# Block two's mixer takes its Fourier half first, then k and v, then q in two halves; the first loads and block one's convolution change order too

## The chip, the cores and the metric

The kernel runs on one core of one Trainium2 chip. The metric is the device time in microseconds (us), the median of several runs. A profile of one execution shows, for each engine, when each instruction ran. The engines are TensorE (PE for its matmuls, PEld for its weight loads), VectorE (DVE), ScalarE (ACT), GpSimd (POOL) and SyncE (SP, which here only issues transfers).

## The reference

256 tokens of width 1024 go through two blocks of two layers each, in float32:

```python
for l in range(2):                                   # block one
    x = x + 0.5 * swiglu_ffn(rmsnorm(x), ...)
    x = x + mixer(rmsnorm(x), ...)                   # GLU + 31-tap convolution + layer norm, three kinds of windowed attention, gates
    x = x + 0.5 * swiglu_ffn(rmsnorm(x), ...)
    x = rmsnorm(x)
for l in range(2):                                   # block two
    p = rmsnorm(x) @ w_in                            # u (512), q (8 heads of 64), k and v (2 heads each)
    y_f = real(fft2(u)) @ w_f + b_f
    y_a = windowed_gqa(rope(rmsnorm(q)), rope(rmsnorm(k)), v, sink)
    x = x + concat(rmsnorm(y_f), rmsnorm(y_a)) @ w_o
    up = conv3(rmsnorm(x) @ w_up)
    x = x + (silu(gate) * val) @ w_down
```

## The kernel before, in words

**Weights as a stream of units.** All weights lie in HBM in the order in which they are used, cut into units of 128 x 1024 (`weight_stream`, `make_units`). `fetch` issues a unit's transfer on SP's queue into one of four `raw` buffers. `ahead` splits a unit in two float32r parts: `wh`, a copy by ACT (line 334), and `wl`, the rest, by DVE (line 335), up to three units ahead of use. `unit` hands the next one out. Each product is three matmuls: `wl` with the high part of the activations, `wh` with the high part, `wh` with the low part.

**Products.** `token_major` computes 256 tokens x 512 columns: four units, and in each two blocks of 128 rows for two token tiles, so 48 matmuls of 512 columns into two PSUM banks (`acc`, a pool of four banks). `mid` is a dictionary: after unit q the functions in `mid[q]` are traced. `evac` is called for token tile 0 and then for tile 1. A second pool of four banks (`aux`) takes transposes, sums, scores. The FFN's products are the same (`ffn1`): `gate(c - 1)` after a product's second unit, its transposes (`turn`) after the fourth, and in the second product the sums of squares (`norm`) after the first unit.

**Order of the work.** The program is traced in Python order, and a scheduler then orders each engine's queue at compile time by what it expects to be ready; each engine works through its queue in order. `issue_after(ins)` keeps what is traced inside it, on the engine of `ins`, behind `ins` in that queue (no wait for its end).

**Start.** `run` issues the transfers of x's eight blocks, with four units in between, and 8 warm-up matmuls. `add(b)` splits block b of x (ACT `xh`, DVE `xl`) and adds its square to a sum (`square_add`: ACT squares, DVE adds). `ahead(-2)` splits one unit behind block 0.

**Block one's mixer.** 13 products of `token_major`: four for the GLU, nine for q, k, v of the three groups. `evac` of q and k reads a PSUM bank (line 868) and runs `head_norm_rope` at once (eight squares with accumulator reads on ACT, a `pow` on POOL, four DVE operations of 512 columns), then the other tile does the same. The transposes of a product follow one product later. The convolution stands between the products: `conv_forward` (lines 786 to 799; three `acc` banks per half), `conv_inverse` (lines 809 to 819; two `acc` banks per half), then mean and variance. Then ten steps of attention with sixteen half units of the gates between them; in each step `scores` (line 897) come first, and `norm_mean`, `norm_cols`, `norm_rows` stand behind steps 1, 3 and 4. Temporaries of 512 columns (`t2`) share nine buffers; bias rows (`brow`) are among them.

**Block two's mixer (`mixer2`).** First q, by `token_major` (`evac_q`, `head_norm_rope` for each tile with eight heads); then u by `token_major`, with the residual's normalisation (`residual`, eight DVE operations, line 1389) after its second unit; then k and v, 48 matmuls of 256 columns (lines 1079 to 1081). Then `f1` (the Fourier transform over the tokens, two halves), the transposes of q and k (`transpose_to`, line 667), and four steps of attention, each with one head of keys and one token tile: `soft` issues the scores (line 1207) and the softmax, `fill` gives what is put between (`f2`, `f3`, the output projection `proj`).

## Time and profile before

| | us |
|---|---|
| median of 3 runs | 1929.17 |
| lowest and highest run | 1925.79, 1930.48 |
| the profiled execution | 1923.16 |
| its span, first to last instruction | 1921.4 |
| mean granted TensorE clock (1 is 2.4 GHz) | 0.996 |

The profile page lists each engine's busy time and the costliest groups of instructions; the trace behind it gives every instruction's start, duration and the idle time of its engine ahead of it, with the instruction whose end released it. Times in rows count from the start of the span. L335 is line 335 of the kernel.

### The profile page before, as it was taken

The numbers are of one execution on the slowest core, as the hardware profiler recorded it, in microseconds if no ns is written. First come the engines' busy times: TensorE is split into PE (matmuls) and PEld (weight loads), VectorE is DVE, ScalarE is ACT, GpSimd is POOL, SyncE is SP. The second block draws the span as 40 slices with busy tenths as digits, with TensorE's granted clock in tenths as the row PEclk, the third lists the DMA queues.
The fourth block names the chain that finished last, engine by engine and source line by source line (L and its number), as shares of the span: only waits on it lengthen the run. The fifth ranks groups of instructions, "written<-read, shape, count | busy, mean of one in ns | idle before, by whom it ended". The sixth has DMA issues, their size and how long they took to land.

```text
span 1921.4 us, 29776 instructions
## 1 busy us (share of the span) xinstructions
PE 1893.8 (99%) x11240; PEld 1656.0 (86%) x11240; DVE 1344.3 (70%) x2232; ACT 1105.9 (58%) x2087; POOL 116.8 (6%) x109
## 2 busy tenths in 40 slices
PE   8999999999999999999999999999989999999999
PEld 6888878899988888888788999888879998879999
DVE  5655687967655566656879776655779985679873
ACT  5554545666544555545457575444677664677652
POOL 1000012300000000000123000000100000100000
PEclk8999999999999999999999999999999999999999
DMA  7655655434555555546555345556434655425553
GB/s 231 218 192 182 212 181 171 163 112 165 187 186 185 183 193 182 196 178 210 182 174 161 122 158 183 187 186 210 136 123 144 213 201 193 165 100 175 197 179 120
DMA packets 95792, 337.99 MB, mean 176 GB/s; under 512 B 11270, under 2 KB 13926, under 8 KB 95520
## 3 DMA queue, kind: packets, MB, share of 16 engines
q1 hardware_dynamic: 91584, 325.97, 49.5%
q0 software_dynamic: 2944, 8.11, 1.8%
q10 hardware_dynamic: 1120, 2.00, 0.3%
q8 instruction: 88, 1.44, 0.3%
q14 instruction: 56, 0.46, 0.1%
HBM read 334.99 MB, written 1.05 MB: 175 GB/s over the span
## 4 chain that ended last, share of the span: by engine, by line
PE 84%; issue 8%; DVE 4%; POOL 2%; DMA 1%; ACT 1%; ACTq 0%; POOLq 0%; DVEq 0%
PE acc L683 11%; PE acc L685 10%; PE acc L684 10%; PE acc L352 10%; PE acc L354 9%; PE acc L353 9%; PE acc L513 5%; PE acc L515 5%; PE acc L514 5%; POOL rs L643 2%; PE pt L1018 1%; PE ht L592 1%; DVE wl L335 1%; PE s L897 1%; PE acc L1169 1%
## 5 line engine op out<-in xcount | busy, mean ns | idle before, releaser
L335 DVE TENSOR_TENSOR wl<-raw,wh 128x1024 fp32r<-128x1024 f32 (+1 forms) x618 | 749.2, 1215 | 405.4 <-ACT wh L334 404.6
L334 ACT ACTIVATE wh<-raw 128x1024 fp32r<-128x1024 f32 (+1 forms) x618 | 647.7, 1052 | 574.9 <-PE acc L685 269.3
L683 PE MATMUL acc<-wl,xh 128*128 128x512 f32 x1184 | 470.3, 397 | 6.6 <-DVE wl L335 4.1
L685 PE MATMUL acc<-wh,xl 128*128 128x512 f32 x1184 | 463.0, 391 | 0.0
L684 PE MATMUL acc<-wh,xh 128*128 128x512 f32 x1184 | 462.1, 390 | 0.0
L683 PEld LDWEIGHTS acc<-wl,xh 128*128 128x128 f32 x1184 | 223.3, 189 | 54.1 <-DVE wl L335 4.9
L685 PEld LDWEIGHTS acc<-wh,xl 128*128 128x128 f32 x1184 | 222.9, 188 | 48.0 <-DVE xl L364 0.2
L684 PEld LDWEIGHTS acc<-wh,xh 128*128 128x128 f32 x1184 | 223.6, 189 | 44.2
L513 PE MATMUL acc<-wl,hh 128*128 128x512 f32 x440 | 172.4, 392 | 0.0
L352 PE MATMUL acc<-xn,wl 128*128 128x256 f32 x608 | 172.1, 283 | 0.0
L353 PE MATMUL acc<-xn,wh 128*128 128x256 f32 x608 | 172.1, 283 | 0.0
L354 PE MATMUL acc<-xn,wh 128*128 128x256 f32 x608 | 172.1, 283 | 0.0
L515 PE MATMUL acc<-wh,hl 128*128 128x512 f32 x440 | 171.3, 389 | 0.0
L514 PE MATMUL acc<-wh,hh 128*128 128x512 f32 x440 | 171.2, 389 | 0.0
L352 PEld LDWEIGHTS acc<-xn,wl 128*128 128x128 f32 x608 | 116.7, 192 | 0.0
L353 PEld LDWEIGHTS acc<-xn,wh 128*128 128x128 f32 x608 | 116.7, 192 | 0.0
L354 PEld LDWEIGHTS acc<-xn,wh 128*128 128x128 f32 x608 | 116.7, 192 | 0.0
L352 PE MATMUL acc<-xh,wl 128*128 128x256 f32 x352 | 103.8, 295 | 0.0
L353 PE MATMUL acc<-xh,wh 128*128 128x256 f32 x352 | 100.1, 284 | 0.0
L354 PE MATMUL acc<-xl,wh 128*128 128x256 f32 x352 | 100.0, 284 | 0.0
L515 PEld LDWEIGHTS acc<-wh,hl 128*128 128x128 f32 x440 | 82.6, 188 | 17.4
L514 PEld LDWEIGHTS acc<-wh,hh 128*128 128x128 f32 x440 | 82.7, 188 | 16.7
(278 smaller groups left out, 2969.2 us busy)
## 6 DMA issues: line engine op xcount, KB each, us to landing
raw<-wts SPq DMA_DIRECT2D x606, 512.0 KB, 3.3
brow<-b_in POOLq DMA_DIRECT2D x26, 256.0 KB, 3.9
raw<-wts SPq DMA_DIRECT2D x8, 384.0 KB, 3.3
fw<-dft SPq DMA_DIRECT2D x4, 512.0 KB, 5.7
tab<-tab ACTq DMA_DIRECT2D x1, 1024.0 KB, 8.4
out<-xn SPq DMA_DIRECT2D x8, 128.0 KB, 3.4
wraw<-conv_w POOLq DMA_DIRECT2D x6, 124.0 KB, 4.7
raw<-dft SPq DMA_DIRECT2D x2, 258.0 KB, 2.6
```

The lines of the kernel that those rows point to most:

```text
L334: nc.scalar.activation(h[:, :n], r[:, :n], AF.Copy)
L335: nc.vector.tensor_tensor(lo[:, :n], r[:, :n], h[:, :n].bitcast(F32), op=ALU.subtract)
L352: mm(out, wl, xh, start=start, stop=False, **k)
L353: mm(out, wh, xh, start=False, stop=False, **k)
L354: mm(out, wh, xl, start=False, stop=stop, **k)
L513: mm(accs[t], hh[:, ts], wl[:, c], start=k == 0, stop=False)
L514: mm(accs[t], hh[:, ts], wh[:, c], start=False, stop=False)
L515: mm(accs[t], hl[:, ts], wh[:, c], start=False, stop=k == NF - 1)
L643: nc.gpsimd.tensor_tensor(rs[:, :nh], vv[:, :nh], self.mhalf[:, :nh], op=ALU.pow)
L683: mm(accs[t], xh[k][:, ts], wl[:, c], start=k == 0, stop=False)
L684: mm(accs[t], xh[k][:, ts], wh[:, c], start=False, stop=False)
L685: mm(accs[t], xl[k][:, ts], wh[:, c], start=False, stop=k == KB - 1)
```

## The change

Block two's mixer: the first product is u, with the sums and the tables' transfer inside; then k and v, both token tiles in one `aux` bank (`product`), with `f1` behind them; then q in two halves of 256 columns (key head 0, key head 1), each again a `product` of 48 matmuls of 256 columns, with `f2` inside the first. `norm_rope` norms and rotates both token tiles at once (one square on ACT, one `tensor_reduce` on DVE, one `pow`), `turn` transposes both tiles into one bank. `f3(0)`, `f3(1)` and the transposes of k and of q's first half stand ahead of the attention; `f3(2)`, `f3(3)` are step 0's fill, q's second transposes step 1's. The residual goes to step 4, behind the last softmax on DVE. The weight stream is reordered to match.

Elsewhere: 14 warm-up matmuls; an ACT table load at the very start; units 1 and 2 split between x's blocks; the squares of x behind the first product's third unit; `norm` and `gate(0)` one unit later in every FFN's second product; what `mid` issues on TensorE pinned behind the unit's last matmul; in block one's mixer both tiles read out of PSUM before either is normed, `conv_forward`'s first two accumulators and `conv_inverse`'s two in `aux`, the norm's sums in `acc`, a gate ahead of the first scores, and the convolution's norm one and two steps later, on DVE and ACT behind the step's softmax.

```diff
-WARM = 8
+WARM = 14
...
-        parts += [_wide(w[:, 512:1024]), _wide(w[:, :512]), w[:, 1024:].reshape(2, 4, P, 256).transpose(0, 2, 1, 3)]
+        parts += [_wide(w[:, :512])] + [w[:, c:c + 256].reshape(2, 4, P, 256).transpose(0, 2, 1, 3) for c in (1024, 512, 768)]
...
     def follow(self, x, gains, scales=(None,)):
-        def add(b):
+        def add(b, both=True):
             for dst, part in zip(o, self.operand(x[b:b + 1], gains[b:b + 1], b)):
                 dst += part
+            if both:
+                square(b)
+
+        def square(b):
             for i, sc in enumerate(scales):
                 sums[i] = self.square_add(sums[i], x[b], **({} if sc is None else dict(scale=sc[b])))
...
     def ffn1(...)
-            mid = {0: tail} if c == 0 else {1: [lambda: gate(c - 1)], 3: [lambda: turn(c - 1)]}
+            mid = {2 if first else 0: tail} if c == 0 else {1: [lambda: gate(c - 1)], 3: [lambda: turn(c - 1)]}
             if c == 1:
-                mid[0] = [norm]
+                mid = {1: [norm], 2: [lambda: gate(0)], 3: [lambda: turn(0)]}
...
     def token_major(self, o, evac, mid={}):
-            for f in mid.get(q, ()):
-                f()
+            if q in mid:
+                with self.tc.issue_after(last.ins):
+                    for f in mid[q]:
+                        f()
-        for t in range(2):
-            evac(t, accs[t])
+        for f in [evac(t, accs[t]) for t in range(2)]:
+            if f is not None:
+                f()
...
     def conv_forward():
-                    a = self.acc()
+                    a = self.acc() if len(parts) == 2 else self.aux("U")
     def conv_inverse(half):
-            parts = [self.acc(), self.acc()]
+            parts = [self.aux("inv"), self.aux("inv")]
...
         def norm_mean():
+            with self.tc.issue_after(stat["soft"].ins), self.tc.issue_after(stat["exp"].ins):
...
                 z = self.t2("z")
                 nc.vector.scalar_tensor_tensor(z, a, r[:, t:t + 1], row, op0=ALU.mult, op1=ALU.add)
                 i = which * 3 + g
-                self.head_norm_rope(z, NH, cg[:, t, i], sg_[:, t, i], z)
                 turn.append(lambda d=dst: self.transpose_to(z, 4, d, t))
+                return lambda: self.head_norm_rope(z, NH, cg[:, t, i], sg_[:, t, i], z)
...
-        later = {1: norm_mean, 3: norm_cols, 4: norm_rows}
+        later = {2: norm_mean, 5: norm_cols, 6: norm_rows}
         for i in range(len(steps) + 2):
+            if i == 0:
+                gate(*gates.pop(0))
+                for f in held:
+                    f()
             if i < len(steps):
                 j, t = steps[i]
                 soft0 = (j, t, soft(t, scores(t, j)))
             gate(*gates.pop(0))
-            if i == 0:
-                for f in held:
-                    f()
...
     def mixer2(...)
+        def product(mid={}):
+            xh, xl = o
+            a = self.aux("pr")
+            for u in range(2):
+                wh, wl = self.unit(1024)
+                for kk in range(4):
+                    k = u * 4 + kk
+                    c = slice(kk * 256, (kk + 1) * 256)
+                    for t in range(2):
+                        out, ts = a[:, t * 256:(t + 1) * 256], slice(t * P, (t + 1) * P)
+                        mm(out, xh[k][:, ts], wl[:, c], start=k == 0 and t == 0, stop=False, skip_group_check=True)
+                        mm(out, xh[k][:, ts], wh[:, c], start=False, stop=False, skip_group_check=True)
+                        last = mm(out, xl[k][:, ts], wh[:, c], start=False, stop=k == KB - 1, skip_group_check=True)
+                if u in mid:
+                    with self.tc.issue_after(last.ins):
+                        for f in mid[u]:
+                            f()
+            return a
+
+        def norm_rope(z, nh, i, out, dup=1):
...
+            nc.scalar.activation(sq, z, AF.Square)
+            nc.vector.tensor_reduce(ss, heads(sq), axis=mybir.AxisListType.X, op=ALU.add)
...
+            nc.gpsimd.tensor_tensor(rs, vv, self.mhalf[:, :n], op=ALU.pow)
...
+            tt(A_, A_, B_, op=ALU.add)
...
+                tt(o4[:, :, u], heads(A_), rs[:, :, None].to_broadcast([P, n, HD]), op=ALU.mult)
+
+        def turn(z, dst):
+            p = self.aux("tr")
+            for i in range(2):
                 for t in range(2):
+                    nc.tensor.transpose(p[:, i * 256 + t * P:i * 256 + (t + 1) * P], z[:, t * 256 + i * P:t * 256 + (i + 1) * P], self.ident)
+            nc.scalar.activation(dst, p.rearrange("p (i c) -> p i c", i=2), AF.Copy)
...
+        def resid():
+            with self.tc.issue_after(cell["soft"]):
+                x.extend(residual())
+
+        fill = {0: [lambda: f3(2), lambda: f3(3)], 1: [lambda: turns[2](), later("s", lambda: self.square_sum([yf[:, b] for b in range(4)]))],
+                2: [lambda: proj(0, 0, 0), later("c", lambda: self.rms_cols(cell["s"], 512))], 3: [lambda: proj(0, 0, 1)],
+                4: [lambda: (fourier_part(0), proj(0, 1, 0)), resid], 5: [lambda: proj(0, 1, 1)]}
...
+        self.token_major(o, lambda t, a: self.split(a, uh[t], ul[t], st["rc"][:, t:t + 1]), {0: tail, 2: [tables], 3: [start]})
+        a = product({1: [lambda: f1(0), lambda: f1(1)]})
...
+        norm_rope(z[:, :256], 2, 1, zk, dup=2)
+        turns = [lambda: turn(zk, kT[:, :2])]
+        for i, mid in enumerate(({0: [lambda: f2(0)], 1: [lambda: f2(1)]}, {})):
+            a = product(mid)
+            zq = self.t2("z")
+            nc.scalar.activation(zq, a, AF.Copy)
+            norm_rope(zq, 4, 0, zq)
+            turns.append(lambda i=i, zq=zq: turn(zq, qT[:, i * 2:i * 2 + 2]))
+        f3(0)
+        f3(1)
+        for f in turns[:2]:
             f()
...
     def run(self):
         nc.scalar.dma_start(self.vec[:, :KB], self.a["vec"][:, :KB])
+        nc.scalar.activation(self.small("tbl", 1), self.mhalf[:, :1], AF.Copy)
...
         for b in range(KB):
-            if b == 1:
-                self.ahead(-2)
-            add(b)
+            add(b, False)
+            if b % 2 and b < 6:
+                self.ahead(b // 2 - 2)
```

## Rows read from the trace of the kernel before

**Rows 1.** Page: busy us (share) xinstructions; two groups: busy, mean ns, idle before.

```profile
PE 1893.8 (99%) x11240; PEld 1656.0 (86%) x11240; DVE 1344.3 (70%) x2232; ACT 1105.9 (58%) x2087; POOL 116.8 (6%) x109
...
L335 DVE TENSOR_TENSOR wl<-raw,wh 128x1024 fp32r<-128x1024 f32 (+1 forms) x618 | 749.2, 1215 | 405.4 <-ACT wh L334 404.6
L334 ACT ACTIVATE wh<-raw 128x1024 fp32r<-128x1024 f32 (+1 forms) x618 | 647.7, 1052 | 574.9 <-PE acc L685 269.3
```

**Rows 2.** Timeline, TensorE, behind `conv_inverse`, layer 0: start, duration, [idle before <-releaser].

```profile
305.61 0.39 PE L685 MATMUL acc<-wh,xl 128*128 128x512 f32 x1
307.11 0.50 PE L683 MATMUL acc<-wl,xh 128*128 128x512 f32 x1 [1.11 <-DVE z L868]
307.45 0.39 PE L684 MATMUL acc<-wh,xh 128*128 128x512 f32 x1
307.68 0.40 PE L685 MATMUL acc<-wh,xl 128*128 128x512 f32 x1
```

**Rows 3.** Timeline, TensorE, inside k and v's product.

```profile
1388.62 0.28 PE L1079 MATMUL acc<-wl,xh 128*128 128x256 f32 x1
1388.74 0.28 PE L1080 MATMUL acc<-wh,xh 128*128 128x256 f32 x1
```

**Rows 4.** Timeline of the first 24 us (q behind an engine: it issues).

```profile
1.05 3.78 PE L1358 MATMUL warm<-ones 128*128 128x128 f32 x16 [1.05 <-DVE ones L242]
...
7.52 0.50 PE L683 MATMUL acc<-wl,xh 128*128 128x512 f32 x1 [2.69 <-DVE wl L335]
...
8.06 15.29 SPq L322 DMA_DIRECT2D raw<-wts  x7
...
15.06 1.01 PE L433 MATMUL sumc<-ones,sacc 128*128 128x1 f32 x4 [2.93 <-DVE sacc L383]
...
17.47 0.79 PE L683 MATMUL acc<-wl,xh 128*128 128x512 f32 x1 [1.40 <-DVE wl L335]
```

**Rows 5.** Windows, first product: length, busy (instructions) by engine, PEclk, DMA share, GB/s.

```profile
7.52:27.76 20.24, 15.92 (x52) 12.62 (x53) 12.49 (x21) 10.74 (x19) 4.05 (x5) 0.75 0.80 259
```

**Rows 6.** Groups of TensorE, 262 to 402 us (block one's mixer, layer 0).

```profile
L683 PE MATMUL acc<-wl,xh 128*128 128x512 f32 x126 | 50.2, 398 | 1.3 <-DVE z L868 1.1 <-DVE yt L797 0.2
...
L897 PE MATMUL s<-qkv,qkv 64*128 64x128 f32 (+1 forms) x60 | 6.9, 329 | 2.3 <-ACT qkv L668 1.9 <-ACT pT L1020 0.4
...
L786 PE MATMUL acc<-uh,wl 128*128 128x512 f32 (+1 forms) x8 | 3.5, 440 | 0.9 <-DVE Y L794 0.7 <-DVE qkv L865 0.2
```

**Rows 7.** Groups of TensorE, 1377 to 1420 us (block two's mixer, layer 0).

```profile
L1079 PE MATMUL acc<-wl,xh 128*128 128x256 f32 x16 | 4.6, 289 | 0.9 <-DVE wl L335 0.9
...
L352 PE MATMUL acc<-yfh,wl 128*128 128x256 f32 x12 | 3.4, 291 | 2.7 <-ACT yfh L360 2.7
...
L667 PE MATMUL tr<-ident,zk 128*128 128x128 f32 x4 | 0.8, 293 | 2.0 <-DVE zk L660 2.0
```

**Rows 8.** Groups of TensorE, 1670 to 1700 us (block two's mixer, layer 1).

```profile
L352 PE MATMUL acc<-yfh,wl 128*128 128x256 f32 x16 | 4.7, 304 | 1.1 <-ACT yF L1135 1.1
...
L667 PE MATMUL tr<-ident,zk 128*128 128x128 f32 x4 | 0.8, 287 | 0.9 <-DVE zk L660 0.9
```

**Rows 9.** DMA issues, first 20 us: count, KB each, median us to landing.

```profile
raw<-wts SPq DMA_DIRECT2D x8, 512.0 KB, 6.5
```

**Rows 10.** Timeline, an FFN's second product: its sums, and `gate(0)`'s two results.

```profile
516.72 0.50 PE L433 MATMUL sumc<-ones,sacc 128*128 128x1 f32 x4
...
519.80 0.88 DVE L585 SCALAR_TENSOR_TENSOR f<-acc,rc,t 128x256 f32<-128x256 f32 x2 [0.57 <-ACT t L584]
```

**Rows 11.** Windows, one product in block one's mixer (columns as in rows 5).

```profile
339.00:350.00 11.00, 11.00 (x52) 9.12 (x51) 11.00 (x17) 6.75 (x24) 3.89 (x3) 1.00 0.71 228
```

**Rows 12.** Groups of ACT, 1650 to 1700 us: the copy of q's transposes.

```profile
L668 ACT ACTIVATE qT<-tr 128x512 f32<-128x512 f32 x2 | 1.1, 618 | 0.0
```

**Rows 13.** Timeline, TensorE, block two's mixer, layer 1.

```profile
1677.50 1.14 PE L1207 MATMUL s<-kT,qT 64*128 64x256 f32 x8
...
1683.57 0.60 PE L1018 MATMUL pt<-ident,e 128*128 128x128 f32 x4
```

106 lines of the change are left out of this document (49 added, 57 removed).

## The prediction

> **What bounds the kernel now.** I read the page's busy times first: TensorE is busy 1893.8 of 1921.4 us [rows 1]. So the end is set by how many matmuls there are and by the few places where TensorE stands still. A matmul's duration in a row is padded, so I take its price from the distance of two starts: 0.23 us for 512 columns [rows 2], 0.12 us for 256 [rows 3]. The change removes no matmul. It can give only idle time, the time after a wait in which matmuls start slowly, and the time at the lower clock. So the second view was TensorE's groups with their idle column, stretch by stretch, and the third the timeline at the start. There are three such places.
>
> The start: the warm-up ends at 4.8, the first product begins at 7.52, stops for 2.93 us for a sum of squares (`sumc`) and for 1.40 us more for `wl` [rows 4]. Its 48 matmuls and the sum's 4 take 20.24 us, with a mean granted clock of 0.75 [rows 5].
>
> Block one's mixer, each layer: idle time in front of `L786`, `L683` and `L897` [rows 6]. The reader is to see who ends it: a DVE evacuation (`L865`, `L794`, `L797`, `L868`), so a PSUM bank was missing, and an ACT copy of transposes that were issued just before (`L668`).
>
> Block two's mixer, each layer: idle time in front of k's transposes, `L1079` and `f3` [rows 7, 8].
>
> **The idle column understates a wait.** From 305.61 to 307.11 a matmul that should follow after 0.23 follows after 1.50, so 1.27 are lost where the column says 1.11; and the one behind it follows after 0.34, not 0.23 [rows 2]. I add 0.27 per wait.
>
> **The change, part by part. The start.** Now the sum of squares stands on TensorE's queue ahead of unit 1, because it was expected to be ready sooner, and ACT's and DVE's squares stand ahead of the next splits. The change puts the squares behind the third unit of the first product, pins what `mid` issues on TensorE behind the unit's last matmul, and splits units 1 and 2 between the blocks of x. What is late next is the weights' transfer. The fourth unit is issued at 8.06 [rows 4]; with a landing 6.5 us later [rows 9] it is there at 14.6. ACT's half of its split takes 1.05 and DVE's 1.22 [rows 1], so it is ready at 16.9, and about 0.6 later as an estimate, since the last two x blocks are split ahead of it on both engines. From 17.5, 12 matmuls at 0.23 end at 20.2. Before they end at 27.76, and the sum of 0.50 [rows 10] is still to be paid: 27.76 - 20.2 - 0.5 = 7.1; I take **7.0**. Bounds: 7.7 without the 0.6; and 0 if the product runs at the lower clock again (36 matmuls at 0.46, twice 0.23, cost 8.3 more, of which the gaps between units take about 1).
>
> The clock: a mean of 0.75 is about half of the stretch at the lower of its two levels (1.2 GHz, not 2.4), and the stretch follows one idle time of 2.69 us and holds one of 2.93 [rows 4, 5]. With 14 warm-up matmuls in place of 8 at 3.78 / 8 = 0.47 us each, the warm-up lasts to about 7.7, and no idle time over about 1 us is left before the product's end; from that I take the upper level. The Trainium skill ("TensorE: Matmul & The Clock Gate", Part 1) has it that the throttled state is the default and that activity releases it; the stretch at 0.75 agrees. By that rule too the sum would be 7.0; by the clock as this trace had it in the old product, some 4 less.
>
> The ACT table load in front costs nothing: unit 0 waits for its weights and x block 1, not for ACT. It stands ahead of four of x's transfers on ACT's queue and waits only for a memset. Should it hold them, x is later by at most its own length, and the fourth unit still is last.
>
> `norm` and `gate(0)` move back one unit in all four FFNs. From the sums to the last `f` are 520.68 - 516.72 = 4.0 us [rows 10]; after, two units (24 x 0.23 = 5.5) cover them before the transposes. 1.5 us to spare: cost 0. Without that cover TensorE would wait for what exceeds it, four times.
>
> **Block one's mixer.** Idle in layer 0 is 0.9 + 1.3 + 2.3 = 4.5 us in six waits [rows 6]; with 0.27 each 6.1. Layer 1 has the same waits but for the one of 0.4: 5.4. Together 11.5. The edits meet each cause: two of `conv_forward`'s three accumulators and `conv_inverse`'s two go to the other four banks; both token tiles are read out of PSUM before the first one's norm; a gate of 24 matmuls (2.9 us) runs between the transposes and the scores that need them. What speaks for less: DVE is busy 11.00 of 11 us from 339 to 350 [rows 11], and with TensorE ahead of where it was, DVE's rope and the last transposes have that much less room. I take **10.0**, bounds 3 (only the wait of 1.1 goes, in each layer) and 11.5. `norm_mean` one step later and the sums two steps later cost nothing as long as the normed convolution is there before its projection; if it isn't, that projection waits. The matmuls that go to other banks cost the same.
>
> **Block two's mixer.** Layer 0 stands idle 0.9 + 2.0 + 2.7 = 5.6 us in four waits [rows 7], 6.7 with their tails; layer 1 0.9 + 1.1 in two [rows 8], 2.5. Together 9.2. After it, u is first, and k/v's two units (48 x 0.12 = 5.8 us) lie over its split; q's halves lie over k's norm, `f1`'s copies and `f2`; the residual's eight DVE multiplications, which stand ahead of the late `wl` of `L1079`, go behind the last softmax. So these waits go. What comes, per layer:
> - q as 96 matmuls of 256 for 48 of 512: 96 x 0.12 - 48 x 0.23 = 0.5 us.
> - The scores now follow right behind the transposes of k and q's first half, and wait for a copy of 0.62 us [rows 12], unless `f3(2)` is put between: 0.6.
> - The first softmax. In layer 1 its scores start at 1677.50 and the transposes of its result at 1683.57: 6.1 us [rows 13]. Between them the new order has `f3(2)`, `f3(3)` (24 x 0.12 = 2.9), two sets of scores (1.06 each) and four transposes (0.60 padded, 0.45 by starts): 5.5. Exposed: 0.6.
>
> That is 1.7 per layer, 3.4 in all: 9.2 - 3.4 = **5.8**. Bounds: 8.2 if only q's split is paid; and a loss of 1.0 if the first softmax is covered by the scores alone (6.1 - 2.1 = 4.0 exposed), beside the 0.5 and the 0.6 in each layer.
>
> ACT's and DVE's work falls here (one square of 512 columns for 16 of 64 with their accumulator reads per pair of tiles); they aren't the bound, so this counts for nothing beyond the waits above. Units are read in another order, the same number.
>
> **Sum.** 7.0 + 10.0 + 5.8 = 22.8 us. The profiled execution took 1923.16 us (span 1921.4 and 1.8 around it): 1900.4. The median of the runs is 1929.17, 6.0 above it, so there I expect **1906.4**.
>
> **The rivals.**
> 1. *DVE is what TensorE waits for.* The banks come free sooner, but splits and rope then come late in block one's mixer, and block two's first softmax stays open. For it: the 11.00 of 11 us [rows 11]. Against it: `wl` ends no wait in this stretch [rows 6]. Gain 7 + 4 + 1 = 12: 1911.2, 1917 as a median.
> 2. *The first product runs at the lower clock.* The gaps between units bring it down. For it: the mean of 0.75 before [rows 5]. Gain 22.8 - 7.0 = 15.8: 1907.4, 1913 as a median. The Trainium skill's page on TensorE (Part 1) would put this down to too little activity between units; no row here shows these gaps.
> 3. *Slower: a pool runs dry.* With both tiles read out first, block one's mixer holds two bias rows, two z that wait for transposes, two new z and `sq`, `ra`, `rb`: all nine of the 512-column buffers. The next bias row's DMA then waits on POOL, with the norm's `pow` behind it, and a product's evacuation waits for its bias. 18 products (9 per layer) pay. It decides from 22.8 / 18 = 1.27 us each; with 2 us it gives 36 - 22.8 = 13.2 more than before: 1936.4, 1942 as a median. Against it: a row is asked for two products (22 us) ahead.
> 4. *No change.* The new order waits at other places for the same things, as an instruction that is expected to be ready and isn't stops a queue as before. 1920 to 1925 in the profile.
>
> **How the numbers follow.** Forecast 0.53, rival 1 0.22, rival 2 0.13, rival 3 0.05, rival 4 0.07. Faster by over 0.3% (5.8 us, about what three runs here can tell from no change: they span 4.7): 0.53 + 0.22 + 0.13 = 0.88; within 0.3%: 0.07; slower: 0.05. The range takes in the forecast's own bounds of 7.7 + 11.5 + 8.2 = 27.4 (1902) with 1 us of scatter, and rivals 2 and 1 (1913, 1917) with 3: 1901 to 1920.
>
> **What would show it.** Start: no `sumc` before the first product's end, `L683` of the second product at about 20.2, clock near 1 from 8 on. Mixer one: no idle at `L786` nor at the first `L683` behind `conv_inverse`, and the first `L897` without one. Mixer two: idle under 2 us per layer, at the first `pt` and `s`. The prediction is wrong if new idle time over 2 us stands at `pt`, `f1` or behind `brow`, or if `wl` becomes a releaser in mixer one.

## The result, and the profile after

The changed kernel took 1902.30 us in the median of four runs (1901.87 to 1904.46), against 1927.48 for the kernel before in the same comparison (1922.43 to 1930.48): a ratio of 0.9874, with a 95% interval of 0.985 to 0.9898. It is faster by 25 us. The profiled execution was the longest of the four, 1904.46 us with a span of 1902.5; set against the profiled execution of before (span 1921.4) it gained 18.9. A second set of runs of the same kernel (`after_again`, below) gave 1901.95, and its profile a span of 1899.9: 21.5 gained.

The table gives where, as the difference of the times at which TensorE begins each stage in two traces:

| us gained | predicted | first profile | second profile |
|---|---|---|---|
| start, to the end of the first FFN's up products | 7.0 | 4.51 | 7.13 |
| block one's mixer, layer 0 | 5.3 | 5.62 | 5.62 |
| block one's mixer, layer 1 | 4.7 | 5.44 | 5.45 |
| block two's mixer, layers 0 and 1 | 5.8 together | 3.07 and 0.27 | 3.01 and 0.27 |
| all else | 0 | 0.0 | 0.0 |

(The prediction's 10.0 for block one's mixer is shared out here as its 6.1 and 5.4 were.) Only the start differs between the two profiles.

The page of the first profile, in answer to [rows 1]: DVE's work is the same, and TensorE's busy time fell a little.

```profile
PE 1888.5 (99%) x11348; PEld 1656.3 (87%) x11348; DVE 1343.7 (71%) x2244; ACT 1099.5 (58%) x2010; POOL 118.0 (6%) x107
```

The start, to compare with [rows 4]: TensorE's timeline in the second profile, its instructions with a wait, up to the end of the first product. The sums are no longer inside; three waits for `wl` are left.

```profile
1.05 5.83 PE L1416 MATMUL warm<-ones 128*128 128x128 f32 x28 [1.05 <-DVE ones L242]
7.51 0.50 PE L688 MATMUL acc<-wl,xh 128*128 128x512 f32 x1 [0.62 <-DVE wl L335]
...
11.56 0.50 PE L688 MATMUL acc<-wl,xh 128*128 128x512 f32 x1 [1.00 <-DVE wl L335]
...
14.86 0.50 PE L688 MATMUL acc<-wl,xh 128*128 128x512 f32 x1 [0.28 <-DVE wl L335]
```

Windows of the second profile, the first product (columns as in [rows 5]): 12.93 us for 20.24, the clock at 1.00 for 0.75, and the transfers busy for 0.94 of it (327 GB/s) where they were at 0.80 (259).

```profile
7.51:20.44 12.93, 11.65 (x49) 8.96 (x50) 9.82 (x15) 10.43 (x19) 0.00 (x0) 1.00 0.94 327
```

The first profile has two more waits behind the start, which the second has not: at the sums, and at 60.23.

```profile
27.15 0.61 PE L438 MATMUL sumc<-ones,sacc 128*128 128x1 f32 x4 [0.93 <-DVE sacc L383]
...
60.23 0.50 PE L688 MATMUL acc<-wl,xh 128*128 128x512 f32 x1 [0.96 <-DVE wl L335]
```

Block one's mixer, layer 0, groups of TensorE in the first profile, for [rows 6]: nothing is left in front of the products, the forward transform or the scores.

```profile
L688 PE MATMUL acc<-wl,xh 128*128 128x512 f32 x134 | 53.2, 397 | 0.0
...
L911 PE MATMUL s<-qkv,qkv 64*128 64x128 f32 (+1 forms) x60 | 6.4, 325 | 0.0
...
L1033 PE MATMUL pt<-ident,e 128*128 128x128 f32 x24 | 3.1, 274 | 0.2 <-DVE e L926 0.2
...
L799 PE MATMUL U<-uh,wl 128*128 128x512 f32 x4 | 1.7, 417 | 0.0
```

Block two's mixer, layer 0, the same view, for [rows 7]: the four old waits are gone, three new ones stand in their place. Layer 1 has the last two of them again (0.55 and 1.02).

```profile
L688 PE MATMUL acc<-wl,xh 128*128 128x512 f32 x9 | 3.7, 413 | 0.5 <-ACT xh L363 0.5
...
L1033 PE MATMUL pt<-ident,e 128*128 128x128 f32 x24 | 3.5, 283 | 1.0 <-DVE e L1272 1.0
...
L1125 PE MATMUL tr<-ident,z 128*128 128x128 f32 x8 | 1.3, 279 | 0.5 <-DVE mx L1255 0.5
```

### The profile page after: what moved, and what is told of

Its sections match the earlier page's. It is cut to its first block, busy times and chain, and to the rows that moved or that the text cites. A ratio compares the mean times of both kernels' runs of the same rounds, so it can differ in the third digit from the quotient of the medians.

```text
span 1902.5 us, 29935 instructions
## 1 busy us (share of the span) xinstructions
PE 1888.5 (99%) x11348; PEld 1656.3 (87%) x11348; DVE 1343.7 (71%) x2244; ACT 1099.5 (58%) x2010; POOL 118.0 (6%) x107
## 3 DMA queue, kind: packets, MB, share of 16 engines
q0 software_dynamic: 2944, 8.11, 1.9%
HBM read 334.99 MB, written 1.05 MB: 177 GB/s over the span
## 4 chain that ended last, share of the span: by engine, by line
PE 90%; DVE 5%; POOL 2%; DMA 1%; issue 1%; ACT 1%; SPq 0%; POOLq 0%; DVEq 0%; ACTq 0%
PE acc L688 12%; PE acc L690 12%; PE acc L689 12%; PE acc L352 9%; PE acc L354 9%; PE acc L353 9%; PE acc L520 5%; PE acc L518 5%; PE acc L519 5%; DVE wl L335 2%; PE pt L1033 1%; POOL rs L648 1%; PE ht L597 1%; PE Y L936 1%; PE s L911 1%
## 5 line engine op out<-in xcount | busy, mean ns | idle before, releaser
L688 PE MATMUL acc<-wl,xh 128*128 128x512 f32 x1152 | 456.1, 396 | 4.6 <-DVE wl L335 4.1
L690 PE MATMUL acc<-wh,xl 128*128 128x512 f32 x1152 | 449.4, 390 | 0.0
L689 PE MATMUL acc<-wh,xh 128*128 128x512 f32 x1152 | 448.4, 389 | 0.0
L688 PEld LDWEIGHTS acc<-wl,xh 128*128 128x128 f32 x1152 | 216.4, 188 | 49.7 <-DVE wl L335 5.6
L690 PEld LDWEIGHTS acc<-wh,xl 128*128 128x128 f32 x1152 | 216.1, 188 | 46.7 <-DVE xl L364 0.6
L689 PEld LDWEIGHTS acc<-wh,xh 128*128 128x128 f32 x1152 | 216.6, 188 | 43.0
```

The source lines that it names most:

```text
L688: mm(accs[t], xh[k][:, ts], wl[:, c], start=k == 0, stop=False)
L689: mm(accs[t], xh[k][:, ts], wh[:, c], start=False, stop=False)
L690: last = mm(accs[t], xl[k][:, ts], wh[:, c], start=False, stop=k == KB - 1)
```

## The experiments

Twelve kernels, each the changed kernel with the edit shown; `...` marks a cut. Times are medians; "the second product at" is the start of its first matmul, 20.44 in the second profile.

### Is what was given back behind the start the kernel's own?

**after_again**: no edit.

> The changed kernel once more, unaltered. Theory A (the waits of 0.93 at 27.15 and of 0.96 at 60.23 come from transfers that landed late in the execution that was profiled, the longest of its four): this profile shows the second product at 20.3 to 20.8 again, but less than 0.5 us of those two waits together, a span near 1900.2, and a median of 1902 to 1902.5. Rival B (they belong to the kernel's own order): both waits are there again, with a span near 1902.5. What stays the same in either case are the four waits of block two's mixer at the second half's transposes of q (0.54) and at the first transposes of e (1.05).

Measured: 1901.95 us (1901.77 to 1902.04), second product at 20.44, neither wait. Theory A held: the two waits do not come in every execution. They are not confined to one either. Two later profiles with the same start have one of them: exp_early_later_gate waits 1.54 us at the sums (27.70), q_whole_banks_evac 0.51 us at 58.39. The rows of ACT in the first profile say how: its splits stand behind a weights' transfer and, later, behind the taps' table, which follows a table of 1 MB.

```profile
24.44 1.06 ACT L334 ACTIVATE wh<-raw 128x1024 fp32r<-128x1024 f32 x1 [2.52 <-DMA raw<-wts]
...
56.41 0.51 ACT L713 ACTIVATE tapf<-traw 96x360 fp32r<-96x360 f32 x1 [7.42 <-DMA traw<-taps]
```

In the second profile ACT waits there too, 1.82 and 6.04 us, and TensorE doesn't: the work that TensorE has meanwhile (the cover) is enough, but only just.

**tables_late**: the tables are computed one product behind their transfers.

```diff
...
-[lambda: prep.append(between(l))]
+[lambda: prep.append(between(l)), lambda: self.mixer_tables(l, prep[0])]
...
```

(`mixer_tables` holds `rope_tables` and the split of the taps; `mixer_prep` keeps the transfers.)

> The changed kernel in which block one's layer takes the rope tables and the taps' split one product later than the transfers that feed them. Theory A (1.2 us of what was given back is the wait of 0.96 at 60.23: ACT waits 7.42 us and DVE 3.25 us for the tables' transfers, with the weights' splits queued behind): this wait goes and the time falls by about 1.2 us. Rival B (the splits there are late because TensorE runs 5 us earlier against the weights' transfers, whatever stands in between): a wait of about the same length stays or appears within the next 20 us, and the time stays within 0.4 us.

Measured: 1903.17 us (1901.94 to 1905.39). The wait is gone from its profile (span 1899.8), as it is from that of the unaltered kernel; the runs are no shorter and scatter more. Theory A's gain isn't there, and nothing shows rival B's wait either. As the wait is absent without the edit too, the run doesn't tell the theories apart.

**squares_early**

```diff
-            mid = {2 if first else 0: tail} if c == 0 else {1: [lambda: gate(c - 1)], 3: [lambda: turn(c - 1)]}
+            mid = {1 if first else 0: tail} if c == 0 else {1: [lambda: gate(c - 1)], 3: [lambda: turn(c - 1)]}
```

> The changed kernel with the squares of x traced one unit earlier (behind the second unit of the first product, not the third). Theory A (1.2 us of the 2.65 that were given back after the first product are the sum of squares being ready late, because DVE's adds are laid between the splits): the wait of 0.93 in front of the sums at 27.15 goes, and the time falls by about 1.2 us, unless the splits of units 3 and 4 come later by the squares that now stand ahead of them. Rival B (the splits are what is late there, since the transfers of units 6 and 7 land at 24.4 and 25.6): the wait moves to a product's first matmul and the time stays within 0.4 us, or grows by up to 1.5.

Measured: 1902.11 us, second product at 20.71, no wait at the sums. As that wait is absent without the edit too, the run doesn't tell the theories apart. It shows something else: with 14 warm-up matmuls TensorE idled 1.88 us ahead of the product (0.62 in the second profile), the product began at 8.11, and up to 12 us it ran mostly at the lower level of the clock (windows, PEclk third from the end).

```profile
8.00:10.00 2.00, 1.89 (x5) 1.50 (x6) 1.34 (x4) 1.32 (x3) 0.00 (x0) 0.56 1.04 361
10.00:12.00 2.00, 2.00 (x7) 1.57 (x6) 1.39 (x2) 0.98 (x2) 0.00 (x0) 0.58 1.06 377
```

### What makes the 7 us at the start?

**squares_old**

```diff
-            add(b, False)
+            add(b)
...
-                mid = {1: [norm], 2: [lambda: gate(0)], 3: [lambda: turn(0)]}
+                mid = {0: [norm], 1: [lambda: gate(0)], 3: [lambda: turn(0)]}
...
-            tail = self.ffn1(x, o, norm, nxt[2], tail if l else [lambda b=b: add.square(b) for b in range(KB)], [lambda: prep.append(between(l))]
+            tail = self.ffn1(x, o, norm, nxt[2], tail, [lambda: prep.append(between(l))]
```

> The changed kernel with the squares of x back in the first splits, and the sum of squares, gate(0) back at their old units (after units 1 and 2 of the second product). Theory A (the squares in front of the splits cost the wait in the first product): the sums or a split of units 2 and 3 are late again, TensorE stands still for 1 to 3 us before about 25 us, and the four FFNs gain or lose nothing elsewhere; the time grows by 1 to 3 us. Rival B (the placement of the squares does not matter once the order is pinned, and only the split of units 1 and 2 between the blocks of x does): the second product starts within 0.3 us of 20.62, the wait of 0.93 at the sums stays or falls, and the time stays within 0.5 us.

Measured: 1902.10 us (1902.07 to 1902.32), second product at 20.79, no wait at the sums. Rival B held: neither the squares' place nor the sums' unit is worth anything by itself.

**start_pinned**: as squares_old, and the splits where they were (shown against the changed kernel).

```diff
-            add(b, False)
-            if b % 2 and b < 6:
-                self.ahead(b // 2 - 2)
+            if b == 1:
+                self.ahead(-2)
+            add(b)
```

> As the run with the old start, with the pin kept, which by itself holds the sums behind the second product's first unit. Theory A (the sums' place is most of the 7 us): the second product starts within 1 us of 20.6 and the time is that of the changed kernel within 1 us. Rival B (the late splits are most of it, since units 2 to 4 are now split behind all eight blocks of x and their squares): TensorE waits 2 to 5 us for wl in the first product, the second starts at 23 to 26, and the time is 3 to 5 us longer.

Measured: 1908.96 us (1908.47 to 1909.71), second product at 27.56. It differs from squares_old by the three lines alone, and by 6.8 us. Rival B held and was still too small: it had the product's end at 23 to 26. TensorE's one wait inside the product, and DVE's queue in front of it:

```profile
17.67 0.65 PE L688 MATMUL acc<-wl,xh 128*128 128x512 f32 x1 [3.33 <-DVE wl L335]
```

```profile
15.54 0.42 DVE L383 TENSOR_TENSOR sacc<-sacc,sq 128x256 f32<-128x256 f32 x1
16.39 4.63 DVE L335 TENSOR_TENSOR wl<-raw,wh 128x1024 fp32r<-128x1024 f32 x4 [0.43 <-ACT wh L334]
```

Four units are split in a row once the last block of x and its square are done. Set against the second profile, the 7.1 us are in three places: the product begins 2.3 later (9.84 for 7.51), the waits inside it are 2.0 longer (3.33 for 1.00 and 0.28), and its matmuls are 2.7 slower, since the granted clock was 0.76 from 7.40 to 14.30 and 0.54 from 17.67 to 20.00. So undoing the splits brings the lower level back with 14 warm-up matmuls, and here it costs time.

**start_old**: as start_pinned, and the first two products without the pin, which puts the sums behind the first unit again.

```diff
-            st[c] = self.token_major(o, None, mid)
+            st[c] = self.token_major(o, None, mid, not (first and c < 2))
...
-                with self.tc.issue_after(last.ins):
+                with self.tc.issue_after(last.ins) if pin else ExitStack():
```

> The changed kernel with its start as before but for the 14 warm-up matmuls: all early splits but one behind x's eight blocks, the squares inside them, sums and gate(0) one unit earlier, and the first two products of the first FFN without the pin. Compiled so, TensorE's queue has the sums behind the first product's first unit again. Theory A (the 7 us at the start are the place of the sums in TensorE's queue and the late splits; the warm-up counts for nothing): the wait of 2 to 3 us at the sums is back, the second product starts at 26 to 28 in place of 20.6 and the time is 4 to 7 us longer than the changed kernel's, even with 14 warm-up matmuls. Rival B (the warm-up or what else changed at the start makes most of it): the second product starts before 23.

Measured: 1909.78 us (1908.87 to 1910.10), second product at 28.03. Theory A's size held, a little above its range, but half of its cause fell beside the run before: with the sums in the product or not, the loss is 7.1 us at the end of the span. The wait only changes its name:

```profile
15.86 1.01 PE L438 MATMUL sumc<-ones,sacc 128*128 128x1 f32 x4 [5.23 <-DVE sacc L383]
18.27 0.79 PE L688 MATMUL acc<-wl,xh 128*128 128x512 f32 x1 [1.40 <-DVE wl L335]
```

**warm8**

```diff
-WARM = 14
+WARM = 8
```

> The changed kernel with 8 warm-up matmuls in place of 14. Theory A (the longer warm-up holds TensorE's clock at its upper level, as the prediction had it): the warm-up ends near 4.8 again, TensorE idles about 2.6 us before the first product, and part of the first product runs at the lower level; 48 matmuls at 0.46 in place of 0.23 would cost 11 us less what the waits for weights hide, so the second product starts at 24 to 27 in place of 20.62 and the time grows by 3 to 6 us. Rival B (the level follows the product itself, which no longer stands still for 2.9 us): the granted clock is 1.0 from the first product on, the second product starts within 0.5 us of 20.62 and the time stays within 0.5 us.

Measured: 1902.38 us (1902.17 to 1902.88), second product at 20.59. Theory A had the clock right and rival B the time. TensorE idles 2.97 us ahead of the product, which begins at full speed, falls to the lower level at about 9 us and is back at about 12 (windows, PEclk third from the end):

```profile
7.80:10.00 2.20, 2.20 (x7) 1.75 (x8) 1.23 (x3) 1.45 (x3) 0.00 (x0) 0.76 1.09 377
10.00:12.00 2.00, 2.00 (x6) 1.50 (x5) 1.45 (x2) 0.91 (x2) 0.00 (x0) 0.50 0.99 353
12.00:14.00 2.00, 2.00 (x9) 1.68 (x9) 0.94 (x3) 1.78 (x3) 0.00 (x0) 0.91 1.04 401
14.00:20.59 6.59, 6.59 (x31) 5.21 (x29) 6.04 (x9) 6.12 (x13) 0.00 (x0) 1.00 0.83 278
```

No loss can be told from scatter: the eight profiles with the start unaltered have the second product at 20.40 to 20.62. The two waits for `wl` inside the product (1.00 and 0.28 at full speed) are gone; the slower matmuls fill them.

### What makes the 11 us in block one's mixer?

**banks_undone**

```diff
-                    a = self.acc() if len(parts) == 2 else self.aux("U")
+                    a = self.acc()
...
-            parts = [self.aux("inv"), self.aux("inv")]
+            parts = [self.acc(), self.acc()]
```

> The changed kernel with the convolution's accumulators all in acc's four banks again (forward and inverse). Theory A (the missing banks are what TensorE waited for there): per layer, the three waits inside the forward transform come back (1.0 us idle, 1.8 with their tails; the stage had gained 2.18) and the wait of 1.11 behind the inverse with it (1.4): together 3.2 to 3.6 per layer, 6.4 to 7.2 us in all. Rival B (reading both tiles out of PSUM first is enough behind the inverse): only the forward transform's part comes back, 3.6 to 4.4 us in all. Rival C (the banks count for nothing now that the evacuations come sooner): under 0.5 us.

Measured: 1907.29 us (1906.93 to 1907.70). Each layer loses 2.1 us in the forward transform, 0.1 in the products behind it and 0.3 by the end of the q, k and v products: 4.9 in all. Rival B held, a little above its range. Layer 0:

```profile
269.62 0.50 PE L799 MATMUL acc<-uh,wl 128*128 128x512 f32 x1 [0.66 <-DVE Y L807]
...
270.82 0.48 PE L799 MATMUL acc<-uh,wl 128*104 128x512 f32 x1 [0.23 <-DVE Y L812]
...
272.62 0.50 PE L688 MATMUL acc<-wl,xh 128*128 128x512 f32 x1 [0.17 <-DVE yt L810]
```

**evac_gate_undone**

```diff
-        for f in [evac(t, accs[t]) for t in range(2)]:
-            if f is not None:
-                f()
+        for t in range(2):
+            f = evac(t, accs[t])
+            if f is not None:
+                f()
...
-            if i == 0:
-                gate(*gates.pop(0))
-                for f in held:
-                    f()
             if i < len(steps):
                 j, t = steps[i]
                 soft0 = (j, t, soft(t, scores(t, j)))
             gate(*gates.pop(0))
+            if i == 0:
+                for f in held:
+                    f()
...
-            if i % 2 == 0 and i > 0:
+            if i % 2 == 0:
```

> The changed kernel with two edits of block one's mixer undone, which act at different places: each tile is normed right behind its own evacuation, and the first gate stands behind the first scores again. Theory A (each of them removes its own wait): the wait of 1.11 behind the inverse comes back (1.4 us per layer) and, at the first scores, the waits of 2.3 us (2.2 to 2.6 with tails): 7 to 8 us in all. Rival B (the banks alone had removed the wait behind the inverse): only the first scores wait, 4.3 to 5.2 us in all. Rival C (the earlier evacuations also carry the forward transform): waits there too, more than 8 us.

Measured: 1904.46 us (1903.50 to 1906.00). No wait behind the inverse. Layer 0 is 0.3 us shorter than with the edits, layer 1 2.05 longer, at the scores. It is rival B's cause, at less than half its size. In layer 1 TensorE waits for the copy of transposes that it issued at 1031.23:

```profile
1038.02 0.49 PE L912 MATMUL s<-qkv,qkv 64*128 64x128 f32 x4 [2.46 <-ACT qkv L673]
```

and ACT's queue says why: the copy stands behind the first softmax, for whose maxima ACT waited 7.25 us, and behind a split.

```profile
1035.02 0.72 ACT L923 ACTIVATE e<-e,m 128x512 f32<-128x512 f32 x1 [7.25 <-DVE m L921]
...
1036.45 1.04 ACT L334 ACTIVATE wh<-raw 128x1024 fp32r<-128x1024 f32 x1
1037.39 0.58 ACT L673 ACTIVATE qkv<-tr 128x512 f32<-128x512 f32 x1
```

**q_whole_banks_evac**: the banks and the evacuation as in the two runs above, and in block two (the weights' order follows):

```diff
-        for i, mid in enumerate(({0: [lambda: f2(0)], 1: [lambda: f2(1)]}, {})):
-            a = product(mid)
+        aq = self.token_major(o, None, {1: [lambda: f2(0)], 3: [lambda: f2(1)]})
+        for i in range(2):
             zq = self.t2("z")
-            nc.scalar.activation(zq, a, AF.Copy)
+            for t in range(2):
+                nc.scalar.activation(zq[:, t * 256:(t + 1) * 256], aq[t][:, i * 256:(i + 1) * 256], AF.Copy)
```

> Two edits of the changed kernel undone at places far apart, so that each stage's own time tells them apart: in block two's mixer q is one product of 512 columns again (its norm still in two halves, behind it); in block one's mixer the convolution's banks and the evacuation are both as before. Block two's mixer, theory A (the halves cost 0.5 us a layer in matmuls and are worth more, because the first half's norm, about 6 us from the product's end to its transposes, lies over the second half's 48 matmuls): TensorE waits 2 to 3.5 us more at the transposes in front of the scores, so each layer is 1.5 to 3 us longer. Rival A (the norm is hidden by f3 and the rest anyway): each layer is 0.5 us shorter. Block one's mixer, theory B (banks or early evacuation, either one alone removes the wait behind the inverse, which is why undoing the one or the other cost nothing there): with both undone the wait of 1.11 is back, 1.2 to 1.5 us a layer beside the 2.1 of the forward transform. Rival B (something else removed it): under 0.4 behind the inverse.

Measured: 1912.16 us (1910.90 to 1916.05). Block one: 2.2 per layer in the forward transform, and the wait behind the inverse is back, 1.4 per layer: theory B held. (Layer 0 as a whole loses 2.6, since its attention is 1.1 shorter than with the edits.) Block two: layer 0 is 0.7 us longer, layer 1 1.5: theory A's sign at half its size, but not its mechanism. At q's first transposes there is no wait, at its second ones 0.32 us for 0.54, at the first transposes of e 1.36 for 1.04 and 1.01. The largest new wait is another one, 0.91 in each layer for `yF` in front of `f3`. In this run `f2(1)` stands behind the product's last unit, with `f3` right behind it. With the 0.27 that the prediction adds per wait it is 1.2 us. As an estimate, without it layer 0 would be 0.5 shorter and layer 1 0.3 longer than with the halves. So it is not shown that the halves pay for themselves.

```profile
301.23 0.50 PE L688 MATMUL acc<-wl,xh 128*128 128x512 f32 x1 [1.10 <-DVE z L883]
...
1392.56 0.39 PE L352 MATMUL acc<-yfh,wl 128*128 128x256 f32 x1 [0.91 <-ACT yF L1174]
```

**exp_early_later_gate**: in block one the gate as in evac_gate_undone and

```diff
-        later = {2: norm_mean, 5: norm_cols, 6: norm_rows}
+        later = {1: norm_mean, 3: norm_cols, 4: norm_rows}
...
         def norm_mean():
-            with self.tc.issue_after(stat["soft"].ins), self.tc.issue_after(stat["exp"].ins):
...
```

and in block two

```diff
-            nc.scalar.activation(zq, a, AF.Copy)
+            zc = nc.scalar.activation(zq, a, AF.Copy)
             norm_rope(zq, 4, 0, zq)
+            if i == 0:
+                with self.tc.issue_after(zc.ins):
+                    nc.scalar.activation(self.small("tbl", 1), self.mhalf[:, :1], AF.Exp)
```

> The changed kernel with one edit added in block two's mixer and three undone in block one's, told apart by each stage's own time. Block two's mixer: a small exponential on ACT behind the norm of q's first half, so that the load of ACT's table (1.28 us) no longer stands in the first softmax. Theory A (the wait of 1.05 in front of the first transposes of e is the chain behind the first scores, and the table load is on it): the wait goes or falls under 0.3 and each layer gains 0.9 to 1.3 us. Rival A (DVE, with the weights' splits between the softmax's steps, sets that chain): each layer gains under 0.4. Block one's mixer: the first gate behind the first scores, and the convolution's norm one and two steps earlier and not held behind the softmax. Theory B (the copy of the last transposes stood behind the convolution's squares on ACT's queue, so it is the later norm that removes the wait of 1.9 at the first scores in layer 0, and the first gate alone did it in layer 1): each layer loses 2.0 to 2.6 us. Rival B (the norm's place counts for nothing): layer 0 gains 0.3 and layer 1 loses 2.05, as in the run that undid the first gate.

Measured: 1919.43 us in the median of eight runs (1918.30 to 1921.36). Block one: 6.7 and 6.6 us longer, theory B's cause at three times its size. TensorE waits 4.87 and 4.86 us for the copy of the last transposes. ACT's queue in layer 0:

```profile
360.90 0.78 ACT L382 ACTIVATE sq<-conv 128x256 f32<-128x256 f32 x2
363.48 0.75 ACT L382 ACTIVATE sq<-conv 128x256 f32<-128x256 f32 x2 [1.80 <-DVE conv L846]
364.14 1.04 ACT L334 ACTIVATE wh<-raw 128x1024 fp32r<-128x1024 f32 x1
365.08 0.58 ACT L673 ACTIVATE qkv<-tr 128x512 f32<-128x512 f32 x1
```

The copy stands behind the squares of the convolution, which wait for DVE, and behind a split. The kernel before had the norm and the gate at these places too, and the same queue on ACT:

```profile
369.25 0.42 ACT L382 ACTIVATE sq<-conv 128x256 f32<-128x256 f32 x1 [1.20 <-DVE conv L833]
369.57 1.04 ACT L334 ACTIVATE wh<-raw 128x1024 fp32r<-128x1024 f32 x1
370.52 0.58 ACT L668 ACTIVATE qkv<-tr 128x512 f32<-128x512 f32 x1
```

Its wait was 1.90. Here TensorE is ready for these scores 8.4 us sooner (360.84 for 369.24) and the copy begins 5.4 sooner, so the wait is longer: the old place of the norm costs more in the new order than it did in the old one. Behind the wait TensorE runs at the lower of its two levels, 1.2 GHz (windows, PEclk third from the end):

```profile
365.70:371.00 5.30, 5.29 (x25) 5.06 (x26) 5.23 (x13) 0.83 (x3) 0.00 (x0) 0.50 0.84 240
371.00:374.00 3.00, 3.00 (x25) 3.00 (x24) 2.82 (x8) 2.31 (x5) 0.00 (x0) 0.88 0.24 100
```

By the rule that the Trainium skill states ("TensorE: Matmul & The Clock Gate", Part 1), that throttled is the default state and activity releases it, this is to be expected; the trace agrees.

Block two: 2.2 and 2.0 us longer. The wait at the first transposes of e stays (0.92 for 1.01 in layer 1), a wait of 0.46 at the second ones is new, and so is one of 0.93 at q's first transposes, since the load now stands in front of the square of q's first half. Theory A fell: without the load in it the first softmax isn't ready in time either. No layer gained, so rival A's time fell as well.

### Can block two's new waits be taken away?

**combined**: tables_late and

```diff
+        def behind(name, f):
+            with self.tc.issue_after(cell[name]):
+                return f()
+
-        fill = {0: [lambda: f3(2), lambda: f3(3)], 1: [lambda: turns[2](), later("s", lambda: self.square_sum([yf[:, b] for b in range(4)]))],
-                2: [lambda: proj(0, 0, 0), later("c", lambda: self.rms_cols(cell["s"], 512))], 3: [lambda: proj(0, 0, 1)],
+        fill = {0: [lambda: behind("max0", lambda: f3(2)), lambda: behind("max0", lambda: f3(3))],
+                1: [lambda: turns[2](), later("s", lambda: behind("soft0", lambda: self.square_sum([yf[:, b] for b in range(4)])))],
+                2: [lambda: behind("soft0", lambda: proj(0, 0, 0)), later("c", lambda: self.rms_cols(cell["s"], 512))], 3: [lambda: proj(0, 0, 1)],
...
+            cell.setdefault("max0", sum_.ins)
...
+            cell.setdefault("soft0", last.ins)
```

("max0" is the first softmax's last `se`, "soft0" its last multiplication.) What it was to mend, DVE's queue in the second profile of the changed kernel: the scores are ready at 1391.7, their maxima begin at 1393.27, and splits stand in front of `se` and of `den`.

```profile
1393.27 0.42 DVE L1255 CUSTOM_DVE_ANT_0 e<-s,tab 128x256 f32<-128x256 f32 x1
...
1394.72 1.22 DVE L335 TENSOR_TENSOR wl<-raw,wh 128x1024 fp32r<-128x1024 f32 x1
...
1398.38 1.23 DVE L335 TENSOR_TENSOR wl<-raw,wh 128x1024 fp32r<-128x1024 f32 x1
1399.52 0.17 DVE L1267 TENSOR_TENSOR den<-den,se 128x4 f32<-128x4 f32 x1
```

> The changed kernel with DVE's queue in block two's mixer arranged around the first softmax: the splits and products that f3(2) and f3(3) bring stand behind its maxima, the sum of squares of y_f and the splits that the first output projection brings behind its last multiplication; and block one's tables one product later. Theory A (the first softmax is late because DVE takes weights' splits, splits of y_f and squares between its steps, 1.6 us ahead of the maxima and 1.1 in front of the denominators, as the trace of the changed kernel shows): the wait at the second half's transposes of q (0.54) and the one at the first transposes of e (1.05) go or fall under 0.2 each, each layer gains 1.5 to 2.1 us, and the median is 1898 to 1899.5 against 1902.3. Rival B (the splits are then late themselves): a wait for wl of 0.5 to 2 us takes their place within the next products, and the gain is under 1 us in all. Rival C (POOL's power of q's second half, which DVE waits for, sets the chain): the maxima start no earlier, under 0.5 us in all.

Measured: 1902.17 us (1902.04 to 1903.99) beside 1901.95 for the unaltered kernel in the same comparison. The wait at q's second transposes is gone and the one at the first transposes of e smaller (0.75 and 0.48), but the second set of e is waited for now, 0.58 and 0.59. Layer 1:

```profile
1672.16 1.23 PE L1039 MATMUL pt<-ident,e 128*128 128x128 f32 x8 [0.48 <-DVE e L1284]
...
1676.78 0.41 PE L1039 MATMUL pt<-ident,e 128*128 128x128 f32 x2 [0.59 <-DVE e L1284]
```

Theory A's chain is real: in layer 1 the first maxima begin as soon as the scores are there, at 1665.61 for 1667.15, and from the scores to the first transposes of e it is 7.7 us for 9.8. In layer 0 the maxima begin only 0.5 sooner (1392.75), because DVE now idles in front of them for the sinks, whose transfer POOL issues (1389.68) behind the power of q's second half. So rival C, that POOL sets the chain, has a part there.

```profile
1392.47 0.17 DVE L1057 TENSOR_SCALAR sink<-nsink 128x8 f32<-128x8 f32 x1 [1.62 <-DMA nsink<-sink]
```

The gain isn't there: what DVE puts off for the first softmax it does in front of the second. The waits of these two places are shorter together (1.33 for 1.58 us in layer 0, 1.07 for 1.55 in layer 1), but the layers are not (0.0 and 0.4 us longer); why not stays open. Rival B had the sign, with another instruction as the late one. No version here beats the changed kernel.

## Why the prediction was right, and where its steps failed

The time (1902.3) lies in the range, 4.1 below the forecast of 1906.4, and the sign and the order of the terms are right: 21.5 us in the second profile for 22.8. That the sum came so near is in part luck: block one's mixer gave 1.1 more than forecast and block two's 2.5 less.

**The start: the size right, the cause half wrong.** 7.13 for 7.0, the product's end at 20.44 for 20.2. The unit that paces it is another one, though: the last wait, at 14.86, is for the third unit, and the fourth is split by about 17.0, before TensorE begins it at 17.72. And the step "the sum of squares stands on TensorE's queue ahead of unit 1" names a wait that costs nothing of its own: start_pinned without it loses as much as start_old with it, and squares_old with early splits loses nothing. The split of units 1 and 2 between the blocks of x is the whole term, by the waits and by the clock that falls with them (start_pinned). The releaser in [rows 4] was the last of two things that were late together. ACT's table load was to cost nothing because the fourth unit would still be last. In the second profile x's last block is issued at 8.03 (5.35 before), and ACT waits for it until 14.24 and splits the fourth unit behind it at 14.65 with no wait for that unit's transfer: x was last, not the fourth unit. By the product's end no cost of it shows.

**The clock: the level right in the profile, the condition and the price wrong.** The changed kernel's two profiles have 1.00 in the first product. But the warm-up ends at 6.88 (second profile) and not at 7.7, and 14 matmuls don't always hold the level: in squares_early it fell with them. And the longer warm-up is worth nothing that shows (warm8). Rival 2 and the lower bound of 0 priced 36 matmuls at the lower level at some 7 us. In warm8 and squares_early part of the product runs there, and it ends at 20.59 and 20.71, 0.15 and 0.27 behind the second profile. The price was counted as if no wait were there; the transfers, at 0.94 of their time in the second profile, set the product.

**Sums and gate(0) one unit later: 0, as costed.** The other FFNs take the same time in both kernels; in the first FFN the cover fell short by 0.93 in the first profile, and by 1.54 in exp_early_later_gate's.

**Block one's mixer: 11.1 for 10.0, of 11.5.** The size was a matter of choice between bounds; no wait but 0.23 and 0.51 is left. Which edit meets which wait was partly wrong. The forward transform's waits are the banks (2.1 to 2.2 per layer). The wait behind the inverse is met twice, by the banks and by the early evacuation: each alone is enough, both undone bring back 1.4. The first scores were put down to transposes "issued just before" [rows 6]. They were late for what stood ahead of their copy on ACT's queue: the convolution's squares. So the later norm, which the prediction costed at nothing and credited with nothing, is a part of the cure: with the gate and the early evacuation undone a layer loses 2.05 or nothing, with the gate and the norm undone 6.7 and 6.6. No run undoes the norm alone, or its place without its hold behind the softmax, so the shares stay open. The losses of the runs add up to more than the 11.1 gained: a wait that is given back is longer when TensorE comes to it earlier, as the 4.87 for 1.90 shows.

**Block two's mixer: 3.3 for 5.8.** The 9.2 were removed, all of them. The price was mis-sized in three places:
- The copy in front of the first scores, 0.6 a layer: not there; `f3(2)` lies between.
- The first softmax, 0.6 a layer: 1.02 and 1.05 idle, 1.3 with the 0.27 that the prediction adds per wait. The latency of 6.1 was read in the order of before; in the new one, DVE takes `z` of q's second half, splits of y_f, squares and weights' splits in between, and it is 9.8 (scores at 1393.17, transposes at 1402.96 in the first profile). The cover of 5.5 was wrong too, the other way: the first output projection runs in front of these transposes (from 1394.51 to the wait before 1400.36 in the second profile). The two errors largely cancel, which is luck; 9.8 over a cover of 5.5 would have left 4.3 open.
- Not in the sum: the transposes of q's second half wait 0.54 for a bank in `aux`, which the first maxima free late (releaser `mx`), 0.8 with the 0.27; and 0.46 once in layer 0 at the first product, 0.7 with the 0.27, for a split of x.

With 0.5 a layer for the halves: 9.2 - 2 x (0.5 + 1.3 + 0.8) - 0.7 = 3.3, which is what was measured in both layers together. Which edit of the new order removed which of the old waits no run tells apart.

**The step from the profile to the median** made the difference of 4.1. 6.0 was added because the runs of before lay that far above the profiled one. In the second set of the changed kernel the median is where its profiled run is (1901.95 and 1901.91), and that run lies 1.5 above the 1900.4 that the terms give. The old kernel scatters more: its 32 runs beside the experiments have spans of 1919.9 to 1928.3, with a mean granted clock of 0.994 or 0.995 in twelve of them (1924.8 to 1928.3) and 0.996 to 0.998 in the others (1919.9 to 1927.1); the changed kernel's eight lie within 2.7 us, all at 1.00. That the scatter comes from the old start, where the clock is low, is not shown: start_old and start_pinned, with the old splits, each lie within 1.3 us, and q_whole_banks_evac, with the new start, spans 5.2.

**The rivals.** DVE as the limiter: in block one's mixer it fell. In the window that answers to [rows 11] (TensorE is 7.7 us ahead there, and the fence shows it shifted by 8) DVE is busy 10.16 of 11 us, where it was 11.00, and no wait of TensorE there is for `wl`.

```profile
331.00:342.00 11.00, 11.00 (x52) 9.13 (x51) 10.16 (x16) 6.55 (x30) 3.32 (x4) 1.00 0.55 177
```

In block two this rival has a part: across the first softmax of layer 0 (second profile) DVE is busy 12.61 of 13.5 us.

```profile
1390.50:1404.00 13.50, 11.89 (x72) 8.77 (x72) 12.61 (x51) 11.67 (x33) 0.70 (x2) 1.00 0.39 117
```

A pool that runs dry: no wait of TensorE is put down to a bias row. No change: the new order does wait for new things, as this rival had it, but for 2.1 and 1.6 us of idle time in block two's two layers and for 0.23 and 0.51 in block one's.

## What to carry to other kernels

A releaser in a profile is the last of what was late; before a wait is credited to an edit, ask what would have ended it had that one been early, and what stands ahead of the releaser on its own engine's queue. When an order is changed, a latency read in the old one holds only if the same instructions of the other engines stand between: here a softmax of 6.1 us became 9.8. An edit undone in the new order is not priced as in the old one: a wait of 1.90 came back as one of 4.87. And the offset between a profiled run and the median is one kernel's own: it was 6.0 us before and none in the second set after, so it is not to be carried over without a reason.

## What the runs showed of the hardware that was not expected

The lower level of TensorE's clock cost nothing that could be told from scatter where transfers set the pace: in warm8 and squares_early part of the first product ran there (0.50 and 0.58 from 10 to 12 us), and it ended 0.15 and 0.27 us behind the second profile's. Elsewhere it was dear: in start_pinned slower matmuls make 2.7 of the 7.1 us lost, and behind the waits of 4.87 and 4.86 us in exp_early_later_gate TensorE ran 5.3 us at 0.50, in layers that are 6.7 and 6.6 longer.

ACT's load of a table took 1.28 us. It began 0.02 us behind the end of the activation ahead of it, and the next activation began 0.01 us behind it (timeline of ACT, exp_early_later_gate):

```profile
1670.84 1.28 ACT L1308 ACT_TABLE_LOAD   x1
1672.13 0.20 ACT L1308 ACTIVATE tbl<-mhalf 128x1 f32<-128x1 f32 x1
```

The Trainium skill ("ScalarE: Activation LUTs", What ACT_TABLE_LOAD costs) has the same 1.28 and adds a drain of about 1.38, 2.66 in all, for every switch; here no such time is seen ahead of the load or behind it, and the measurement decides.
